# Four fixed PSUM banks for the seven-product units of an fp32 two-block transformer kernel

## The chip, the cores and the metric

The kernel runs on one core of a Trainium2 chip. The metric is the device time of one launch in microseconds, the median of several runs of the same program. A profile is one further execution, taken with the hardware profiler.

## What the reference computes

Two transformer blocks of width 1024 over 512 tokens, all in fp32. The first has two layers: a stick-breaking attention and a retention, each followed by a squared-ReLU MLP with 4096 hidden units. The second is a gated feed-forward, a mixer (a sparse attention beside an mLSTM), and a second gated feed-forward, each of the two with 2816 hidden units. What matters here are the up projections of these four feed-forward parts:

```python
def squared_relu_mlp(h, w_up, w_down):
    u = jax.nn.relu(h @ w_up)
    return (u * u) @ w_down
...
def swiglu_ffn(x, g, w_gate, w_up, w_down):
    h = rms_norm_2(x, g)
    return (jax.nn.silu(h @ w_gate) * (h @ w_up)) @ w_down
```

## The kernel before

Everything is kept transposed: a tile is 128 features by 512 tokens. An fp32 product is made of three TensorE passes over operands that are split in a high and a low part (`mm3`, L125 to L129: high by low, low by high, high by high), so each weight tile is cast to its high part on ScalarE and its low part is the difference, made on VectorE. The engines' names are those of the profile: PE is TensorE, ACT is ScalarE, DVE is VectorE, SP the queue that issues most transfers, POOL GpSimd.

**Dense units.** `g_unit` (L286) makes one 128 by 512 output tile in one PSUM bank: 8 feature tiles, 3 passes of 512 columns each, 24 matmuls. It takes its bank from the tag `m` (3 banks). Only the first three units of the first gated feed-forward take theirs from the tag `z` (4 banks), which `SPARE = 3` says. The eighth bank has the tag `o` and serves small jobs.

**Seven-product units.** Most of the up projections (groups 1 to 3 of 4 in each MLP, the gate and up pairs 4 to 21 of 22 in each gated feed-forward) are made by Strassen's scheme in Winograd's form: a pair of output tiles with its tokens halved is a 2 by 2 block product, made with seven half-sized products in place of eight. There are 12 such units in each MLP and 18 in each gated feed-forward, 60 in all. `w_unit` (L330) runs one: seven products x = 0 to 6 of 4 feature tiles by 3 passes, so 84 matmuls of 256 columns. The products accumulate on each other. The unit has one bank `a` of tag `m`, with c11 in its left half and p5 in its right half, and one bank of tag `z` with c in its left and b in its right half. Product 0 goes to c11, 1 to p5, 2 to b, 3 to c11, 4 to c, 5 to b, 6 to c. Between products ACT copies partial results, in `between(x)`, which stands after the second of a product's four feature tiles:

- x = 1, L342: b is set to c11 (as it is after product 0), PSUM to PSUM;
- x = 2, L344: p5 is copied to SBUF, as s5;
- x = 3, L346: c is set to b (after product 2), PSUM to PSUM;
- x = 5, L348: c (after product 4) is copied to SBUF, as s3.

At the end the four results are c11, b + s5, c and p5 + s3. `pair_done` (L553 in the MLP, L1002 in the gated feed-forward) takes them out of PSUM four steps after the unit's end (`later`, LAG = 4; a step is half a product of the next unit), applies the nonlinearity and splits the result into high and low parts for the down projection. Units take `z` banks in turn from two that `w_banks` (L296) sets aside at the start of the part, and `m` banks in turn from three. `w_banks` writes each of its banks once with a matmul that starts a group, so that later matmuls without a start flag add to what ACT has put there.

**Weights.** `prep` (L218) is called once a product, after the second feature tile. It casts weights up to five products ahead: ACT writes the high part (L274 for seven-product weights, L242 for dense ones), DVE the low part (L234, L243), and DVE makes two of the sums of weight blocks (L265). The other sums come from transfers that POOL issues with an add.

**Order.** The text of the kernel gives every instruction its priority. The tile framework's planner then lays out each engine's queue and adds the waits, and it moves instructions past each other where one would wait: in the trace the matmuls of one product are interrupted by some of another unit's. Each engine runs its queue in order. An instruction that writes a PSUM bank waits until another engine has finished with that bank.

Of the kernel before, what the change touches and what calls it, by code (L numbers as in the profile page):

```python
# [11 lines left out]
AF = mybir.ActivationFunctionType  # L12
ALU = mybir.AluOpType
# [28 lines left out]
ML = 2  # L42
AT = 2
ZT = 1
SPARE = 3
S1 = 16
S2 = 18
GAS = 1
# [39 lines left out]
class Builder:  # L88
    def __init__(self, tc, d, out, pools):
        self.tc, self.nc, self.d, self.out = tc, tc.nc, d, out  # L90
        self.cp, self.wp, self.hp, self.sp, self.pp = pools
        self.seq = []
        self.subs = []
        self.spare = 0
        self.pend = []
        self.n = 0
        self.pos = 0
        self.raw_at = 0
        self.prep_at = 0
        self.raws = {}  # L100
        self.sums = {}
        self.whi = {}
        self.wraw = set()
        self.ready = {}
        self.uid = 0
        self.stop_at = None
# [178 lines left out]

    def g_unit(self, name, X, w=None):  # L286
        w = w or self.next(name)
        ps = self.ps("z" if self.spare > 0 else "m")
        self.spare -= 1
        n = len(X)  # L290
        for k in range(n):
            self.mm3(ps, w[:, k * 128:(k + 1) * 128], X[k], k == 0, k == n - 1)
            yield
        self.last = ps

    def w_banks(self, any512):  # L296

        out = []
        for _ in range(2):
            b = self.ps("z")  # L300
            self.nc.tensor.matmul(b, self.onesr, any512, start=True, stop=True)
            out.append(b)
        return out

    def w_operands(self, X, T, lift):
# [21 lines left out]
                      "t2": p2[:, lo], "t3": p2[:, hi]})  # L327
            yield

    def w_unit(self, name, T, bank):  # L330


        nc = self.nc
        lo, hi = slice(0, 256), slice(256, 512)
        a = self.ps("m")
        c11, p5, c, b = a[:, lo], a[:, hi], bank[:, lo], bank[:, hi]
        s = self.h()
        s5, s3 = s[:, lo], s[:, hi]

        def between(x):  # L340
            if x == 1:
                nc.scalar.activation(b, c11, AF.Copy)  # L342
            elif x == 2:
                nc.scalar.activation(s5, p5, AF.Copy)  # L344
            elif x == 3:
                nc.scalar.activation(c, b, AF.Copy)  # L346
            elif x == 5:
                nc.scalar.activation(s3, c, AF.Copy)  # L348

        for x, (dst, (_, y)) in enumerate(zip((c11, p5, b, c11, c, b, c), WOPS)):  # L350
            w = self.next(name)
            for k in range(4):
                self.mm3(dst, w[:, k * 128:(k + 1) * 128], T[k][y], x == 0 and k == 0, k == 3, skip=True)
                if k == 1:
                    between(x)
                    self.prep()
                if k % 2:
                    yield
        self.last = (c11, (b, s5), c, (p5, s3))

    def g_tokens(self, name, X, done):

# [176 lines left out]
    def mlp(self, layer, hh, X, box, nxt):  # L539

        nc = self.nc
        st = {}
        self.norm_soon(st, box)
        U = {}


        def up_done(m, ps):
            z = self.h()
            nc.scalar.activation(z, ps, AF.Relu)
            nc.scalar.activation(z, z, AF.Square)  # L550
            U[m] = self.split(z)

        def pair_done(m, p):  # L553
            c11, c12, c21, c22 = p
            lo, hi = slice(0, 256), slice(256, 512)
            y, z = self.h(), self.h()
            nc.vector.tensor_tensor(y[:, hi], c12[0], c12[1], ALU.add)
            nc.vector.tensor_tensor(z[:, hi], c22[0], c22[1], ALU.add)
            nc.scalar.activation(y[:, lo], c11, AF.Relu)
            nc.scalar.activation(z[:, lo], c21, AF.Relu, scale=-1.0)  # L560
            nc.vector.scalar_tensor_tensor(y, y, 0.0, y, ALU.max, ALU.mult)
            nc.scalar.activation(z[:, hi], z[:, hi], AF.Relu, scale=-1.0)
            nc.scalar.activation(z, z, AF.Square)
            U[m] = self.split(y)
            U[m + 1] = self.split(z)

        def down_done(grp, m, ps):
            if "R2" not in st:
                st["R2"] = self.h()
                nc.vector.tensor_tensor(st["R2"], st["R"], st["R"], ALU.mult)  # L570
            t = self.h()
            nc.vector.tensor_tensor(t, ps, st["R2"], ALU.mult)  # L572
            nc.vector.tensor_tensor(hh[m], hh[m], t, ALU.add)
            if grp == 3:
                nxt(m)

        T = []
        ops = self.w_operands(X, T, lambda k: self.lifted(hh[k], self.g(f"mlp{layer}", k)))
        banks = self.w_banks(X[0].hi)

        def main():
            for grp in range(4):
                for m in range(0, 8, 2):
                    if grp == 0:
                        for x in range(2):
                            yield from self.g_unit(f"up{layer}", X[::2] + X[1::2])
                            self.later(up_done, m + x, self.last)
                    else:
                        yield from self.w_unit(f"up{layer}", T, banks[m // 2 % 2])
                        self.later(pair_done, m, self.last)  # L590
                if grp == 0:
                    for _ in ops:
                        pass
                self.flush()
                W = [U[m] for m in range(8)]
                for m in range(8):
                    yield from self.g_unit(f"dn{layer}", W)
                    self.later(down_done, grp, m, self.last)

        self.weave(main(), [[ops, WT]])  # L600
        self.flush()

# [385 lines left out]
    def ffn(self, which, hh, X, st, nxt, lift, after=lambda: None):  # L988
# [3 lines left out]
        U = {}  # L992
# [6 lines left out]
            nc.vector.tensor_tensor(z, pu, z, ALU.mult)  # L999
            U[i] = self.split(z)  # L1000

        def pair_done(i, p):  # L1002
            c11, c12, c21, c22 = p
            R = st["R"]
            lo, hi = slice(0, 256), slice(256, 512)
            z, u = self.h(), self.h()
            nc.vector.tensor_tensor(z[:, hi], c12[0], c12[1], ALU.add)
            nc.vector.tensor_tensor(z[:, lo], c11, R[:, lo], ALU.mult)
            nc.vector.tensor_tensor(z[:, hi], z[:, hi], R[:, hi], ALU.mult)
            nc.scalar.activation(z, z, AF.Silu)  # L1010
            nc.vector.tensor_tensor(u[:, hi], c22[0], c22[1], ALU.add)
            nc.vector.scalar_tensor_tensor(u[:, lo], c21, -1.0, z[:, lo], ALU.mult, ALU.mult)
            nc.vector.scalar_tensor_tensor(u[:, hi], u[:, hi], -1.0, z[:, hi], ALU.mult, ALU.mult)  # L1013
            U[i] = self.split(u)

        def down_add(m, ps, c):
            t = self.h()
# [12 lines left out]
        def main():  # L1030
            for gi, grp in enumerate((range(0, 8), range(8, 16), range(16, 22))):
                for i in grp:
                    if i < GC:
                        yield from self.g_unit(f"gu{which}", X[::2] + X[1::2])
                        pg = self.last
                        yield from self.g_unit(f"gu{which}", X[::2] + X[1::2])
                        self.later(up_done, i, pg, self.last)
                        if i == GC - 1:
                            for _ in ops:
                                pass  # L1040
                            after()
                    else:
                        yield from self.w_unit(f"gu{which}", T, banks[i % 2])
                        self.later(pair_done, i, self.last)
                self.flush()
                W = [U[i] for i in grp]
                tail = gi == 2 and which == 2
                for m in range(7 if tail else 8):
                    yield from self.g_unit(f"fd{which}" if gi < 2 else f"fe{which}", W)
                    self.later(down_done, gi == 2, m, self.last)  # L1050
                if tail:

                    w = self.next(f"fe{which}")
                    for a, b in ((0, 256), (256, 512)):
                        ps = self.ps("m")
                        for k in range(6):
                            self.mm3(ps[:, a:b], w[:, k * 128:(k + 1) * 128], [x[:, a:b] for x in W][k], k == 0, k == 5)
                            yield
                        down_add(7, ps, slice(a, b))
                        nc.sync.dma_start(out=self.out[7][:, a:b], in_=hh[7][:, a:b])  # L1060
# [592 lines left out]
    def build(self):  # L1653
# [121 lines left out]
                nc.vector.scalar_tensor_tensor(hh[kt], hh[kt], self.g("fin", kt), R1, ALU.mult, ALU.mult)  # L1775
        self.later(two_norms, lag=N1)
        self.later(spread_r, lag=N2)
        self.spare = SPARE
        X, Y = [], X
        self.ffn(1, hh, Y, st, ready("mixn", X, hh), lambda k: self.lifted(hh[k], self.gg[:, k:k + 1]), residual)  # L1780
        if stop == "ffn1":
# [162 lines left out]
```

## Time and profile before

| | |
|---|---|
| median of 3 runs | 2537.15 us (2536.19 to 2539.76) |
| the profiled execution, device time | 2539.24 us |
| its span, first to last instruction | 2537.5 us |
| mean granted TensorE clock | 0.997 of full speed |
| PE busy, share of the span | 99% |
| DVE, ACT busy | 68%, 50% |

The profile's PE durations overlap: a matmul's row lasts longer than the time until the next one may start, so a PE that is busy for 99% of the span can still lose time. What a matmul costs is read from the distance between the starts of two neighbours. PE is the matmul itself and PEld the load of its stationary operand, which normally runs ahead of it.

### The profile page before, as it was taken

The numbers are of one execution on the slowest core, as the hardware profiler recorded it, in microseconds if no ns is written. First come the engines' busy times: TensorE is split into PE (matmuls) and PEld (weight loads), VectorE is DVE, ScalarE is ACT, GpSimd is POOL, SyncE is SP. The second block draws the span as 40 slices with busy tenths as digits, with TensorE's granted clock in tenths as the row PEclk, the third lists the DMA queues.
The fourth block names the chain that finished last, engine by engine and source line by source line (L and its number), as shares of the span: only waits on it lengthen the run. The fifth ranks groups of instructions, "written<-read, shape, count | busy, mean of one in ns | idle before, by whom it ended". The sixth has DMA issues, their size and how long they took to land.

```text
span 2537.5 us, 35245 instructions
## 1 busy us (share of the span) xinstructions
PE 2501.1 (99%) x13679; PEld 2148.6 (85%) x13679; DVE 1719.4 (68%) x3061; ACT 1259.9 (50%) x2160; POOL 138.1 (5%) x242
## 2 busy tenths in 40 slices
PE   9999999999999999999999999999999999999999
PEld 7888788888888888888888888888877888889888
DVE  7877856656555555656657766667899677666665
ACT  6777745435333323535536444445556454544443
POOL 0000000010000000000010001010000000001010
PEclk9999999999999999999999999999999999999999
DMA  4112144453322222244352445453221112445451
GB/s 168 67 50 84 67 121 138 116 143 115 109 74 84 87 83 88 83 121 150 114 149 100 128 134 144 148 134 112 71 83 67 67 67 83 111 147 146 147 136 71
DMA packets 78512, 273.20 MB, mean 108 GB/s; under 512 B 8836, under 2 KB 9220, under 8 KB 60680
## 3 DMA queue, kind: packets, MB, share of 16 engines
q1 hardware_dynamic: 60912, 239.43, 26.8%
q0 software_dynamic: 17280, 31.46, 7.5%
q8 instruction: 107, 1.75, 0.3%
q14 instruction: 61, 0.50, 0.1%
q10 hardware_dynamic: 152, 0.06, 0.0%
HBM read 268.82 MB, written 2.10 MB: 107 GB/s over the span
## 4 chain that ended last, share of the span: by engine, by line
PE 91%; DVE 4%; ACT 3%; issue 1%; DMA 0%; SPq 0%; ACTq 0%; DVEq 0%
PE ps_m L127 23%; PE ps_m L128 22%; PE ps_m L129 22%; PE ps_z L127 7%; PE ps_z L129 6%; PE ps_z L128 6%; ACT whi L242 1%; PE ps_z L789 1%; PE ps_z L136 1%; PE ps_z L790 1%; PE ps_o L437 1%; PE ps_z L137 1%; DVE wlo L243 1%; PE ps_o L444 1%; DVE h L1385 0%
## 5 line engine op out<-in xcount | busy, mean ns | idle before, releaser
L127 PE MATMUL ps_m<-h,whi 128*128 128x512 f32 (+1 forms) x2450 | 925.4, 379 | 13.2 <-ACT ps_z L342 3.9
L128 PE MATMUL ps_m<-h,wlo 128*128 128x512 f32 (+1 forms) x2450 | 919.0, 375 | 2.1 <-DVE wlo L234 2.1
L129 PE MATMUL ps_m<-h,whi 128*128 128x512 f32 (+1 forms) x2450 | 917.8, 375 | 0.0
L242 ACT ACTIVATE whi<-raw 128x1024 fp32r<-128x1024 f32 (+2 forms) x297 | 309.8, 1043 | 569.7 <-PE ps_m L129 463.8
L127 PEld LDWEIGHTS ps_m<-h,whi 128*128 128x128 f32 x2450 | 462.4, 189 | 104.1 <-ACT ps_z L342 6.9
L129 PEld LDWEIGHTS ps_m<-h,whi 128*128 128x128 f32 x2450 | 462.2, 189 | 81.4 <-issue 0.2
L128 PEld LDWEIGHTS ps_m<-h,wlo 128*128 128x128 f32 x2450 | 462.8, 189 | 77.9 <-DVE wlo L234 3.2
L243 DVE TENSOR_TENSOR wlo<-raw,whi 128x1024 fp32r<-128x1024 f32 (+2 forms) x297 | 356.8, 1201 | 161.6 <-ACT whi L242 148.3
L274 ACT ACTIVATE wlo<-raw 128x512 fp32r<-128x512 f32 x120 | 75.4, 630 | 175.4 <-PE ps_m L128 128.7
L175 DVE TENSOR_TENSOR h<-h 128x512 fp32r<-128x512 f32 (+1 forms) x172 | 114.8, 685 | 56.3 <-ACT h L174 55.4
L127 PE MATMUL ps_z<-h,whi 128*128 128x256 f32 (+1 forms) x504 | 149.6, 297 | 0.5 <-ACT ps_z L346 0.5
L174 ACT ACTIVATE h<-h 128x512 fp32r<-128x512 f32 (+1 forms) x172 | 105.1, 624 | 88.2 <-DVE h L1013 28.7
L129 PE MATMUL ps_z<-h,whi 128*128 128x256 f32 (+1 forms) x504 | 145.1, 288 | 0.0
L128 PE MATMUL ps_z<-h,wlo 128*128 128x256 f32 (+1 forms) x504 | 144.9, 288 | 0.0
L127 PE MATMUL ps_z<-h,wlo 128*128 128x256 f32 x480 | 141.0, 294 | 0.0
L129 PE MATMUL ps_z<-h,wlo 128*128 128x256 f32 x480 | 135.7, 283 | 0.0
L128 PE MATMUL ps_z<-h,whi 128*128 128x256 f32 x480 | 135.6, 282 | 0.0
L572 DVE TENSOR_TENSOR h<-ps_m,h 128x512 f32<-128x512 f32 x64 | 44.2, 691 | 131.4 <-PE ps_m L129 131.4
L234 DVE TENSOR_TENSOR wlo<-raw,wlo 128x512 fp32r<-128x512 f32 x120 | 82.4, 687 | 49.5 <-ACT wlo L274 48.5
L127 PE MATMUL ps_m<-h,wlo 128*128 128x256 f32 x360 | 105.1, 293 | 4.6 <-ACT ps_z L342 4.5
L127 PEld LDWEIGHTS ps_z<-h,whi 128*128 128x128 f32 x504 | 96.0, 191 | 11.0 <-ACT h L348 6.0
L128 PE MATMUL ps_m<-h,whi 128*128 128x256 f32 x360 | 102.2, 285 | 1.2 <-DVE whi L234 1.2
(346 smaller groups left out, 4138.9 us busy)
## 6 DMA issues: line engine op xcount, KB each, us to landing
raw<-dn SPq DMA_DIRECT2D x32, 1024.0 KB, 4.8
raw<-gu SPq DMA_DIRECT2D x72, 256.0 KB, 3.9
raw<-gu SPq DMA_DIRECT2D x36, 512.0 KB, 4.4
raw<-fd SPq DMA_DIRECT2D x16, 1024.0 KB, 4.8
raw<-up SPq DMA_DIRECT2D x48, 256.0 KB, 3.6
raw<-up SPq DMA_DIRECT2D x24, 512.0 KB, 4.4
raw<-gu POOLq DMA_DIRECT2D x36, 256.0 KB, 4.1
h<-gu SPq DMA_DIRECT2D x36, 256.0 KB, 4.7
```

The costliest lines, as they stand in the source:

```text
L127: mm(ps, lhs.hi, rhs.lo, start=first, stop=False, skip_group_check=skip)
L128: mm(ps, lhs.lo, rhs.hi, start=False, stop=False, skip_group_check=skip)
L129: mm(ps, lhs.hi, rhs.hi, start=False, stop=last, skip_group_check=skip)
L136: mm(ps, stack, rhs.lo, start=first, stop=False)
L137: mm(ps, stack, rhs.hi, start=False, stop=last)
L174: self.nc.scalar.activation(p.hi, x, AF.Copy)
L175: self.nc.vector.tensor_tensor(p.lo, x, p.hi.bitcast(F32), ALU.subtract)
L234: nc.vector.tensor_tensor(lo, src, hi.bitcast(F32), ALU.subtract)
L242: nc.scalar.activation(hi[:, a:b], r[:, a:b], AF.Copy)
L243: nc.vector.tensor_tensor(lo[:, a:b], r[:, a:b], hi[:, a:b].bitcast(F32), ALU.subtract)
L274: self.nc.scalar.activation(t[:, 0:512], src, AF.Copy)
L572: nc.vector.tensor_tensor(t, ps, st["R2"], ALU.mult)
```

## The change

The unit has four banks of tag `z`, one for each of c11 (`a`), p5 (`p`), b and c, of which the left half is used, and the same four serve all units of a part. The tag `m` is left to the dense units. Products 0 and 1 start a group in their own bank, so only b and c need the matmul of `w_banks`. The copies stand ahead of a product's first matmul, in `before(x)`. `pair_done` now returns four functions, of which three run inside the unit: c11 is taken out at x = 4, b + s5 and p5 + s3 at x = 6; the rest (c, the second half of the nonlinearity, both splits) runs one step after the unit's end. `SPARE` is gone, and every dense unit takes a bank of tag `m`.

```diff
     def g_unit(self, name, X, w=None):
         w = w or self.next(name)
-        ps = self.ps("z" if self.spare > 0 else "m")
-        self.spare -= 1
+        ps = self.ps("m")
...
     def w_banks(self, any512):
-        out = []
-        for _ in range(2):
-            b = self.ps("z")
+        out = [self.ps("z") for _ in range(4)]
+        for b in out[2:]:
             self.nc.tensor.matmul(b, self.onesr, any512, start=True, stop=True)
-            out.append(b)
         return out
...
-    def w_unit(self, name, T, bank):
+    def w_unit(self, name, T, banks, done):
         nc = self.nc
-        lo, hi = slice(0, 256), slice(256, 512)
-        a = self.ps("m")
-        c11, p5, c, b = a[:, lo], a[:, hi], bank[:, lo], bank[:, hi]
+        n = slice(0, 256)
+        a, p, b, c = [t[:, n] for t in banks]
         s = self.h()
-        s5, s3 = s[:, lo], s[:, hi]
+        s5, s3 = s[:, n], s[:, 256:512]
-        def between(x):
+        def before(x):
             if x == 1:
-                nc.scalar.activation(b, c11, AF.Copy)
+                nc.scalar.activation(b, a, AF.Copy)
             elif x == 2:
-                nc.scalar.activation(s5, p5, AF.Copy)
+                nc.scalar.activation(s5, p, AF.Copy)
             elif x == 3:
                 nc.scalar.activation(c, b, AF.Copy)
+            elif x == 4:
+                done[0](a)
             elif x == 5:
                 nc.scalar.activation(s3, c, AF.Copy)
+            elif x == 6:
+                done[1](b, s5)
+                done[2](p, s3)
-        for x, (dst, (_, y)) in enumerate(zip((c11, p5, b, c11, c, b, c), WOPS)):
+        for x, (dst, (_, y)) in enumerate(zip((a, p, b, a, c, b, c), WOPS)):
             w = self.next(name)
+            before(x)
             for k in range(4):
-                self.mm3(dst, w[:, k * 128:(k + 1) * 128], T[k][y], x == 0 and k == 0, k == 3, skip=True)
+                self.mm3(dst, w[:, k * 128:(k + 1) * 128], T[k][y], x < 2 and k == 0, k == 3, skip=True)
                 if k == 1:
-                    between(x)
                     self.prep()
                 if k % 2:
                     yield
-        self.last = (c11, (b, s5), c, (p5, s3))
+        self.later(done[3], c, lag=1)
...
-        def pair_done(m, p):
-            c11, c12, c21, c22 = p
+        def pair_done(m):
             lo, hi = slice(0, 256), slice(256, 512)
             y, z = self.h(), self.h()
-            nc.vector.tensor_tensor(y[:, hi], c12[0], c12[1], ALU.add)
-            nc.vector.tensor_tensor(z[:, hi], c22[0], c22[1], ALU.add)
-            nc.scalar.activation(y[:, lo], c11, AF.Relu)
-            nc.scalar.activation(z[:, lo], c21, AF.Relu, scale=-1.0)
-            nc.vector.scalar_tensor_tensor(y, y, 0.0, y, ALU.max, ALU.mult)
-            nc.scalar.activation(z[:, hi], z[:, hi], AF.Relu, scale=-1.0)
-            nc.scalar.activation(z, z, AF.Square)
-            U[m] = self.split(y)
-            U[m + 1] = self.split(z)
+            def d11(c11):
+                nc.scalar.activation(y[:, lo], c11, AF.Relu)
+            def d12(p, q):
+                nc.vector.tensor_tensor(y[:, hi], p, q, ALU.add)
+                nc.vector.scalar_tensor_tensor(y, y, 0.0, y, ALU.max, ALU.mult)
+            def d22(p, q):
+                nc.vector.tensor_tensor(z[:, hi], p, q, ALU.add)
+            def d21(c21):
+                nc.scalar.activation(z[:, lo], c21, AF.Relu, scale=-1.0)
+                nc.scalar.activation(z[:, hi], z[:, hi], AF.Relu, scale=-1.0)
+                nc.scalar.activation(z, z, AF.Square)
+                U[m] = self.split(y)
+                U[m + 1] = self.split(z)
+            return d11, d12, d22, d21
...
-                        yield from self.w_unit(f"up{layer}", T, banks[m // 2 % 2])
-                        self.later(pair_done, m, self.last)
+                        yield from self.w_unit(f"up{layer}", T, banks, pair_done(m))
...
-        self.spare = SPARE
```

The gated feed-forward's `pair_done` is cut in the same way: d11 multiplies c11 by the norm's row (DVE), d12 adds b and s5, multiplies, and takes the Silu of the gate, d22 adds p and s3, and d21 makes the two products of up and gate and the split.

## Rows read from the trace of the kernel before

**Rows 1.** The page: busy time by engine, and the chain that ended last.
```profile
PE 2501.1 (99%) x13679; PEld 2148.6 (85%) x13679; DVE 1719.4 (68%) x3061; ACT 1259.9 (50%) x2160; POOL 138.1 (5%) x242
...
PE 91%; DVE 4%; ACT 3%; issue 1%; DMA 0%; SPq 0%; ACTq 0%; DVEq 0%
```

**Rows 2.** Busy time by stretch: the twelve with seven-product units (three shown), and their sum.
```profile
470.20:516.00 45.80, 44.96 (x345) 42.27 (x344) 30.99 (x48) 30.08 (x60) 1.73 (x2) 1.00 0.42 132
...
1451.50:1497.10 45.60, 44.33 (x345) 41.87 (x344) 37.09 (x64) 26.69 (x50) 1.72 (x2) 1.00 0.42 133
1539.30:1628.90 89.60, 87.30 (x679) 82.59 (x678) 65.69 (x119) 52.47 (x100) 8.63 (x10) 1.00 0.52 151
...
sum 678.80, PE 664.08 PEld 626.57 DVE 481.40 ACT 415.85 POOL 42.08; mean PE 55.34 PEld 52.21 DVE 40.12 ACT 34.65 POOL 3.51
```
A line has the stretch, its length, then busy time (and instructions) of PE, PEld, DVE, ACT and POOL, the granted clock, and the DMA engines' share and rate.

**Rows 3.** Timeline of one unit in the first gated feed-forward: PE and ACT.
```profile
1562.67 0.61 ACT L274 ACTIVATE whi<-raw 128x512 fp32r<-128x512 f32 x1
...
1562.96 0.28 PE L127 MATMUL ps_m<-h,wlo 128*128 128x256 f32 x1
...
1563.19 0.37 ACT L342 ACTIVATE ps_z<-ps_m 128x256 f32<-128x256 f32 x1
...
1563.61 0.38 PE L127 MATMUL ps_m<-h,wlo 128*128 128x256 f32 x1 [0.37 <-ACT ps_z L342]
...
1563.83 0.28 PE L128 MATMUL ps_m<-h,wlo 128*128 128x256 f32 x1
...
1565.73 0.28 PE L129 MATMUL ps_z<-h,whi 128*128 128x256 f32 x1
...
1566.05 0.37 ACT L346 ACTIVATE ps_z<-ps_z 128x256 f32<-128x256 f32 x1 [0.35 <-PE ps_z L129]
...
1566.21 0.28 PE L128 MATMUL ps_m<-h,wlo 128*128 128x256 f32 x1
...
1566.47 0.39 PE L127 MATMUL ps_z<-h,whi 128*128 128x256 f32 x1
...
1566.70 0.28 PE L128 MATMUL ps_z<-h,whi 128*128 128x256 f32 x1
...
1571.03 0.28 PE L128 MATMUL ps_z<-h,wlo 128*128 128x256 f32 x1
...
1573.54 0.28 PE L128 MATMUL ps_m<-h,whi 128*128 128x256 f32 x1
```
A line has start and length in us, engine, line and operation; in brackets the engine's idle time before it and what ended it.

**Rows 4.** Who waited for whom, PEld and PE: us in total, times, longest.
```profile
PEld ps_m L127 <- ACT ps_z L342: 16.1, 37, 0.7
PEld ps_z L127 <- ACT h L348: 11.8, 58, 0.2
PEld ps_z L127 <- ACT ps_z L346: 9.2, 41, 0.7
...
PEld ps_m L127 <- ACT whi L242: 4.4, 10, 0.5
...
PEld ps_m L128 <- DVE wlo L234: 3.2, 6, 0.5
PEld ps_m L128 <- DVE whi L234: 2.7, 7, 0.4
...
PE ps_m L127 <- ACT ps_z L342: 8.4, 23, 0.5
```

**Rows 5.** Groups of DVE instructions in the stretch 470.2 to 516 us.
```profile
L561 DVE SCALAR_TENSOR_TENSOR h<-h 128x512 f32<-128x512 f32 x3 | 2.1, 684 | 0.0
...
L557 DVE TENSOR_TENSOR h<-ps_z,h 128x256 f32<-128x256 f32 x3 | 1.3, 425 | 0.2
```
A line has the count, then busy us and mean ns of one, then the engine's idle us before them.

**Rows 6.** Timeline at the start of the first gated feed-forward: PE and DVE.
```profile
1417.92 0.49 PE L127 MATMUL ps_m<-h,whi 128*128 128x512 f32 x1
...
1420.74 0.68 DVE L997 TENSOR_TENSOR h<-ps_z,h 128x512 f32<-128x512 f32 x1
...
1422.37 0.39 PE L127 MATMUL ps_z<-h,whi 128*128 128x512 f32 x1
```

More of the change, by code (lines that the diff above doesn't have):

```diff
@@ L44 @@
 ZT = 1
-SPARE = 3
 S1 = 16
@@ L93, in __init__ @@
         self.subs = []
-        self.spare = 0
         self.pend = []
@@ L1000, in up_done, with pair_done, d11, d12 @@
             U[i] = self.split(z)
-        def pair_done(i, p):
-            c11, c12, c21, c22 = p
+        def pair_done(i):
+            lo, hi = slice(0, 256), slice(256, 512)
             R = st["R"]
-            lo, hi = slice(0, 256), slice(256, 512)
             z, u = self.h(), self.h()
[L1007 to L1014, printed above, removed]
+            def d11(c11):
+                nc.vector.tensor_tensor(z[:, lo], c11, R[:, lo], ALU.mult)
+            def d12(p, q):
+                nc.vector.tensor_tensor(z[:, hi], p, q, ALU.add)
+                nc.vector.tensor_tensor(z[:, hi], z[:, hi], R[:, hi], ALU.mult)
+                nc.scalar.activation(z, z, AF.Silu)
+            def d22(p, q):
+                nc.vector.tensor_tensor(u[:, hi], p, q, ALU.add)
+            def d21(c21):
+                nc.vector.scalar_tensor_tensor(u[:, lo], c21, -1.0, z[:, lo], ALU.mult, ALU.mult)
+                nc.vector.scalar_tensor_tensor(u[:, hi], u[:, hi], -1.0, z[:, hi], ALU.mult, ALU.mult)
+                U[i] = self.split(u)
+            return d11, d12, d22, d21
         def down_add(m, ps, c):
@@ L1042, in main @@
                     else:
-                        yield from self.w_unit(f"gu{which}", T, banks[i % 2])
-                        self.later(pair_done, i, self.last)
+                        yield from self.w_unit(f"gu{which}", T, banks, pair_done(i))
                 self.flush()
```

## The prediction

> **What bounds the kernel.** I read the page first, then busy time by stretch, a timeline inside one stretch, the table of waits, and last the groups of DVE instructions. By the page the chain that ended last lies on PE for 91% of the span, DVE and ACT together take 7%, and PE is busy for 99% while DVE and ACT have room [rows 1]. So a change pays only where PE loses time between matmuls, and the busy share hides that, because rows of pipelined matmuls overlap. The distance between starts shows it. In an undisturbed run 22 matmuls of 256 columns start between 1571.03 and 1573.54 us: 21 steps of 0.1195 us [rows 3].
>
> The change touches the seven-product units alone, and these lie in twelve stretches (six of four units in the MLPs, in each gated feed-forward one of four, one of eight, one of six), 678.8 us in sum [rows 2]. Their 60 units have 60 x 84 = 5040 matmuls of 256 columns, which need 5040 x 0.1195 = 602 us. Each stretch also holds some seven to ten dense matmuls that the planner moved in (345 in the first row of [rows 2] less 4 x 84 leaves 9), over twelve stretches some 95, which at the distance of 0.23 us that [rows 6] show for 512 columns (1417.92 to 1422.37 in 19 steps) make 22 us. What is left, 678.8 - 602 - 22 = 55 us, is time in which PE started nothing. No gain inside the units can be larger than about 55 us.
>
> **Where the 55 us go.** The timeline shows the two kinds of stop [rows 3]. The large one: ACT begins the copy L342 of c11 at 1563.19, after a weight cast (L274) that began at 1562.67; PE's last start before it is at 1562.96, the next is at 1563.61, when the copy is through. That is 0.65 us in place of 0.12. The matmuls released there are those of product 1, which write p5, a half of the bank that the copy does not read: they wait for the bank, not for data. After such a stop the next load is exposed as well (1563.61 to 1563.83, 0.22 in place of 0.12). One stop costs 0.53 + 0.10 = 0.63 us. The small one: L346 holds back a matmul from 1566.21 to 1566.47, and the next start is at 1566.70: 0.14 + 0.11 = 0.25 us. The planner had put matmuls of another unit ahead of it, so most of the wait was already filled.
>
> The table of waits counts them [rows 4]. L342 stops the load 37 times, and 23 times so long that the matmul row too shows idle time: 23 x 0.63 + 14 x 0.25 = 18 us. L348 (58 times) and L346 (41 times) at 0.25 us: 14.5 + 10.3 = 25 us. Together 43 us by this count. From the other side: late weights (L242, and L234 twice) account for 4.4 + 3.2 + 2.7 = 10.3 us, with 13 exposed loads behind L234 some 11.6 us, and 55 - 11.6 = 43. Both ways are rough by 2 us. I take 42 us for waits on the four copies' banks.
>
> **The change, part by part.**
>
> *Four banks.* A product never writes a bank that is being copied. The copy of c11 to b must be done when product 2 starts, no longer while product 1 runs; c from b is needed by product 4, with product 3 in between; s3 leaves c while product 5 writes b. Each copy gets one product of cover. From the last start of a product to the first start that needs its copy there are 13 steps, 1.55 us. The hand-off takes: last start to copy 0.32 us (1565.73 to 1566.05), copy 0.37 us, and 0.05 us until PE goes on (1566.42 to 1566.47) [rows 3]: 0.74 us. That leaves 0.81 us. A cast in hand at that moment delays the copy by up to 0.61 us (L274): still hidden. Two casts one behind the other, 1.2 us, make PE 0.4 us late, 0.5 with the exposed load. Bounds: all 42 us gone, or half of some 150 copies late by 0.25 us as now, some 20 us left. I take 3 us left, because ACT is busy for 52.5 of 89.6 us in a stretch [rows 2] and the copy stands ahead of the casts of its product in the text.
>
> *Waits that stay.* Nothing removes the 11.6 us of late weights directly. But they come about where the planner has pulled matmuls forward into a stop (a product that is begun early holds its weights' buffers longer, and the casts wait for buffers). With fewer stops to fill, part should go. Bounds 0 and 11.6; I take 4.
>
> *Extraction inside the unit.* The same instructions, moved: none is added or removed on ACT or DVE. They stand ahead of the casts of products 4 and 6 in the text, so on ACT and DVE later casts queue behind them, at most 0.42 + 0.68 + 0.42 = 1.5 us on DVE (L557 twice, L561) [rows 5]. Those casts are for products up to five ahead, more than 7 us of PE time, which hides it; without that cover it would be up to 1.5 us in each of 60 units. No transfer is issued there, and the order on SP's and POOL's queues stays. The pool tiles taken a unit earlier cost nothing unless that pool is empty, and no wait in [rows 4] is on it.
>
> *One set for all units.* This adds waits. The next unit's product 1 starts a group in p, so the DVE read of p + s3 must be over; before, the units took turns among five banks. The read follows product 5: 0.32 us, then the DVE work of 1.5 us, with one cast in hand 0.69 us more (the longest kind, as L561), 2.5 us. Product 1 of the next unit starts after products 6 and 0, 25 steps or 2.99 us. It fits, by 0.5 us. Behind that matmul all of PE would wait. The copy that overwrites b needs the read of b, which comes first, and c and a have two products of room. I take 0 and give the other end as a rival.
>
> *`w_banks` and `SPARE`.* Four calls with two matmuls each, before and after: 0. The first gated feed-forward's fourth dense unit now needs the bank that DVE L997 reads at 1420.74 [rows 6]. There the trace already has a dense unit in `m` at 1417.92 while another waits for a `z` bank until 1422.37. With three `m` banks the third unit starts at about 1417.9 and runs for 24 x 0.23 = 5.5 us, to 1423.4, and L997 ends at 1421.4. So 0; if L997 were later by 4 us, 2 us.
>
> **Sum.** -42 + 3 - 4 = -43 us. The profiled execution took 2539.2 us (1.7 more than its span), so 2496 us in its terms. The median of the runs is 2.1 us lower: 2494 us.
>
> **A rule against it.** DVE is busy for 65.7 us of a stretch of 89.6 [rows 2], so reads can queue, yet no wait of PE on a DVE read of a bank stands in [rows 4]. The Trainium skill, "Perfetto Trace Analysis", section "Matmul Optimizations", asks that all eight PSUM banks be used. By that rule the step from five banks in turn to four fixed ones goes the wrong way, and the time is that of the single-set rival below. The same page, section "Matmuls", lets independent groups rotate through banks so that the evacuation of one overlaps the next; by that the change is right. The trace of before has only PE held up by copies in a shared bank, which is for the second.
>
> **Rivals.**
>
> - *Copies late (chance 0.13).* ACT, or the planner's order on it, puts two casts ahead of a copy often enough that 20 to 30 us of the 42 stay. For it: in [rows 3] the copy L342 did stand behind a cast. Against: one cast is covered. Time: 42 - 20 to 30 + 4 leaves a gain of 16 to 26 us, 2511 to 2521.
> - *Single set, slower (0.05).* The read of p + s3 comes late because DVE has several casts in hand. It costs nothing until DVE is 0.5 us later than worked out, and eats the whole gain when each unit loses 42/60 = 0.7 us more. With four casts of 0.69 us in hand in place of one the read ends at 4.6 us, 1.6 us late, with the exposed load 1.7 in each unit: 60 x 1.7 = 102 us, less 43, about 2595 us; two casts in hand give 0.2 late and 18 us, 2512. Four are unlikely with DVE idle for a quarter of the stretch.
> - *No change (0.06).* PE's time comes back as waits for weights: ACT to DVE to PE becomes the limit. It would need DVE to be busy all the time; 65.7 us for eight units are 8.2 us for a unit that would take 84 x 0.1195 = 10.04. Time: 2537.
> - *Everything (0.04).* The late weights and all stops go: 55 us, 2482.
>
> **How the numbers follow.** The forecast has 0.72, with a range of its own of 2486 to 2508 (a gain of 51: no copy late and 9 of the 11.6 us gone; a gain of 29: 13 us of late copies and none of the 11.6 gone). Left out above 2518 are the two rivals at no change and slower and part of the late copies, 0.15, and below 2484 0.03: the range is 2484 to 2518. A change of 0.2% (5 us) is about what a measurement can tell here. Faster by more: 0.72 + 0.13 + 0.04, that is 0.89; within: 0.05; slower: 0.06.
>
> **What would show it.** Right: the waits on L342, L346 and L348 (by their new lines) nearly vanish from the list of PE and PEld; the stretch of eight units shrinks from 89.6 to about 83 us; matmuls of a product follow each other in order, with no other unit's in between; the stretches' busy time on ACT and DVE stays. Wrong: a wait of PE on a DVE instruction that reads a bank; waits on casts longer than now; casts of 0.61 us directly ahead of most copies with a PE wait behind them; or a loss outside the twelve stretches, above all at the start of the first gated feed-forward.

## The result, and the profile after

The median is 2482.82 us (2482.13 to 2484.37, 4 runs) against 2538.45 us before (2536.19 to 2539.86, 4 runs): the ratio is 0.9783, 95% interval 0.9766 to 0.9799, 55.6 us less. The direction is as forecast, the size is not: the forecast was 2494 us, the range 2484 to 2518, and the time is that of the rival "everything" (2482 us, chance 0.04). The profiled execution took 2483.38 us, with a span of 2481.7 us.

In the changed kernel the lines have moved: the three passes of `mm3` are L125 to L127, the copies L337 (c11 to b), L339 (s5), L341 (b to c) and L345 (s3), the weight casts L272 on ACT and L232 on DVE. The page, busy time and chain:

```profile
PE 2458.5 (99%) x13679; PEld 2141.8 (86%) x13679; DVE 1723.5 (69%) x3061; ACT 1253.1 (50%) x2160; POOL 138.1 (6%) x242
...
PE 93%; DVE 3%; ACT 2%; issue 1%; DMA 0%; SPq 0%; DVEq 0%; ACTq 0%
```

Nothing in the busy shares tells of a gain of 2%: against [rows 1] PE is at 99% both times. The stretches tell it (busy time by stretch, columns as in [rows 2]):

```profile
467.80:508.00 40.20, 40.20 (x337) 40.19 (x335) 32.29 (x51) 30.03 (x62) 1.72 (x2) 1.00 0.47 151
...
1430.00:1471.70 41.70, 40.49 (x338) 40.29 (x337) 37.63 (x67) 26.26 (x51) 1.72 (x2) 1.00 0.46 146
1515.40:1595.90 80.50, 80.50 (x673) 80.50 (x672) 67.35 (x122) 51.57 (x101) 8.63 (x10) 1.00 0.58 167
...
sum 604.60, PE 603.39 PEld 603.08 DVE 497.50 ACT 411.41 POOL 42.09; mean PE 50.28 PEld 50.26 DVE 41.46 ACT 34.28 POOL 3.51
```

The twelve stretches take 604.6 us in place of 678.8 [rows 2]. They no longer hold dense matmuls (336 or 672 of the unit's own, give or take one at the edges), which were 22 us of the 678.8. So the units need 604.6 us where they needed about 657, and 5040 matmuls at 0.1195 us are 602: of the 55 us of stops 52 to 53 are gone. What is left is mostly in the second stretch shown, the first unit of the first gated feed-forward. The list of who waited for whom has one entry of PEld on a copy, where [rows 4] have 136:

```profile
PEld ps_z L125 <- ACT h L345: 1.4, 1, 1.4
```

The waits for late weights inside the stretches are gone as well, and in all twelve stretches the twelve matmuls of each product follow each other with none of another product in between.

The remaining 3 us of the difference between the two spans (55.8) lie outside the stretches and have two sources. One is the end of each stretch: before, a load some 4 us after it waits 0.2 to 0.3 us for the split of the last unit's results (L175, in the changed kernel L173); after, two such waits are left (before, then after; the wait of 0.9 stands elsewhere):

```profile
PEld ps_m L127 <- DVE h L175: 3.9, 13, 0.9
```

```profile
PEld ps_m L125 <- DVE h L173: 0.3, 2, 0.2
```

By the distances between starts in the 10 us behind each stretch this brings 1.6 us in all. The other is the granted clock. From the end of the last stretch of the first gated feed-forward to the first of the second it is 477.2 us before and 475.7 after, and 474.7 and 478.3 in two of the kernels below (`spare0` and `between`). In this part the granted clock falls to 0.50 (the lower level, 1.2 GHz) during or right behind 24 matmuls of 2 columns; the spell lasts 10.2 us before and in `between`, 3.4 us after and in `spare0` (columns as in [rows 2], before, then after):

```profile
1964.20:1974.40 10.20, 10.20 (x33) 8.65 (x33) 6.18 (x15) 2.75 (x5) 0.41 (x2) 0.50 0.00 0
```

```profile
1928.50:1931.80 3.30, 3.30 (x9) 2.54 (x9) 2.58 (x4) 1.85 (x4) 0.41 (x2) 0.50 0.00 0
```

There matmuls of 512 columns start 0.43 us apart in place of 0.23, and by starts the long spell costs 5.0 us, the short one 1.5. Two other spells (near 280 us in both, near 1890 us before and 1850 after) are longer after than before, which takes back 2.1 us. So some 1.4 us of the difference is the clock in the two executions that were profiled, and no run ties it to the change.

One hand-off in the changed kernel (timeline, PE and ACT):

```profile
1546.94 0.28 PE L127 MATMUL ps_z<-h,wlo 128*128 128x256 f32 x1
...
1547.06 0.28 PE L125 MATMUL ps_z<-h,whi 128*128 128x256 f32 x1
1547.17 0.63 ACT L172 ACTIVATE h<-h 128x512 fp32r<-128x512 f32 x1 [0.55 <-DVE h L1027]
...
1547.71 0.37 ACT L337 ACTIVATE ps_z<-ps_z 128x256 f32<-128x256 f32 x1
...
1548.38 0.28 PE L127 MATMUL ps_z<-h,whi 128*128 128x256 f32 x1
1548.50 0.28 PE L125 MATMUL ps_z<-h,wlo 128*128 128x256 f32 x1
```

Product 0 has its last start at 1546.94, product 1 runs on at once, the copy stands behind a 0.63 us ACT instruction and is through at 1548.08, and product 2, which needs it, starts at 1548.50 without a pause, 0.42 us after the copy's end. In [rows 3] the same copy behind the same kind of instruction stopped PE for 0.5 us.

### The profile page after: what moved, and what is told of

The parts are those of the page before. It is cut to its first block, busy times and chain, and to the rows that moved or that the text cites. A ratio compares the mean times of both kernels' runs of the same rounds, so it can differ in the third digit from the quotient of the medians.

```text
span 2481.7 us, 35229 instructions
## 1 busy us (share of the span) xinstructions
PE 2458.5 (99%) x13679; PEld 2141.8 (86%) x13679; DVE 1723.5 (69%) x3061; ACT 1253.1 (50%) x2160; POOL 138.1 (6%) x242
## 4 chain that ended last, share of the span: by engine, by line
PE 93%; DVE 3%; ACT 2%; issue 1%; DMA 0%; SPq 0%; DVEq 0%; ACTq 0%
PE ps_m L125 20%; PE ps_m L126 20%; PE ps_m L127 20%; PE ps_z L125 9%; PE ps_z L127 9%; PE ps_z L126 9%; PE ps_z L134 1%; PE ps_z L796 1%; PE ps_o L437 1%; DVE wlo L241 1%; PE ps_z L135 1%; PE ps_z L797 1%; PE ps_o L444 1%; ACT whi L240 0%; DVE h L1399 0%
## 5 line engine op out<-in xcount | busy, mean ns | idle before, releaser
L125 PE MATMUL ps_m<-h,whi 128*128 128x512 f32 (+1 forms) x2114 | 831.2, 393 | 7.1 <-DVE h L1191 3.5
L126 PE MATMUL ps_m<-h,wlo 128*128 128x512 f32 (+1 forms) x2114 | 826.0, 391 | 0.0
L127 PE MATMUL ps_m<-h,whi 128*128 128x512 f32 (+1 forms) x2114 | 825.0, 390 | 0.0
L125 PEld LDWEIGHTS ps_m<-h,whi 128*128 128x128 f32 x2114 | 398.1, 188 | 89.3 <-issue 6.6
L127 PEld LDWEIGHTS ps_m<-h,whi 128*128 128x128 f32 x2114 | 398.1, 188 | 83.3
L126 PEld LDWEIGHTS ps_m<-h,wlo 128*128 128x128 f32 x2114 | 398.5, 189 | 76.9 <-issue 1.2
L125 PE MATMUL ps_z<-h,whi 128*128 128x256 f32 x840 | 237.8, 283 | 1.2 <-ACT h L345 1.2
L125 PE MATMUL ps_z<-h,wlo 128*128 128x256 f32 x840 | 237.7, 283 | 0.0
L126 PE MATMUL ps_z<-h,wlo 128*128 128x256 f32 x840 | 237.7, 283 | 0.0
L127 PE MATMUL ps_z<-h,whi 128*128 128x256 f32 x840 | 237.7, 283 | 0.0
L127 PE MATMUL ps_z<-h,wlo 128*128 128x256 f32 x840 | 237.7, 283 | 0.0
L126 PE MATMUL ps_z<-h,whi 128*128 128x256 f32 x840 | 237.7, 283 | 0.0
L125 PEld LDWEIGHTS ps_z<-h,whi 128*128 128x128 f32 x840 | 161.2, 192 | 1.8 <-ACT h L345 1.4
L126 PEld LDWEIGHTS ps_z<-h,whi 128*128 128x128 f32 x840 | 161.2, 192 | 0.4
L125 PEld LDWEIGHTS ps_z<-h,wlo 128*128 128x128 f32 x840 | 161.3, 192 | 0.0
L126 PEld LDWEIGHTS ps_z<-h,wlo 128*128 128x128 f32 x840 | 161.3, 192 | 0.0
L127 PEld LDWEIGHTS ps_z<-h,wlo 128*128 128x128 f32 x840 | 161.3, 192 | 0.0
L127 PEld LDWEIGHTS ps_z<-h,whi 128*128 128x128 f32 x840 | 161.2, 192 | 0.0
L272 ACT ACTIVATE wlo<-raw 128x512 fp32r<-128x512 f32 x120 | 75.0, 625 | 148.8 <-PE ps_m L126 127.9
```

What stands on the lines that cost most here:

```text
L125: mm(ps, lhs.hi, rhs.lo, start=first, stop=False, skip_group_check=skip)
L126: mm(ps, lhs.lo, rhs.hi, start=False, stop=False, skip_group_check=skip)
L127: mm(ps, lhs.hi, rhs.hi, start=False, stop=last, skip_group_check=skip)
L272: self.nc.scalar.activation(t[:, 0:512], src, AF.Copy)
```

## Experiments

Two theories stood against each other. *Banks*: PE stops because a matmul waits until another engine has finished with the bank that it writes; four banks take that wait away. *Order*: the earlier place of the copies and the extraction brings the gain. A third question was why the late weights went. All medians stand beside a run of the kernel before on the same chip (2538 to 2540 us); ratios are to that.

**spare0.** The kernel before with one constant changed.

```diff
-SPARE = 3
+SPARE = 0
```

> The kernel before, with the one constant SPARE at 0: all dense units take their bank from the tag of three. If my sum is right, the first three dense units of the first gated feed-forward neither wait nor gain: 2538 us, within 3 us. If the shift of the early units into the other tag was worth the part of the gain that lies outside the seven-product stretches (3 us), it shows here as 2535 us.

Measured: 2537.69 us, ratio 0.9998 (0.9989 to 1.0007). The dropped `SPARE` is worth nothing that can be measured.

**oldbanks.** The changed kernel's order on the old banks.

```diff
-        a, p, b, c = [t[:, n] for t in banks]
+        m = slice(256, 512)
+        left, right = self.ps("m"), banks[0]
+        banks.append(banks.pop(0))
+        a, p, b, c = left[:, n], left[:, m], right[:, m], right[:, n]
```

(with two banks in `w_banks`, and the start flag at product 0 alone)

> The changed kernel's order (copies ahead of a product, extraction inside the unit) on the banks of the kernel before: c11 and p5 share one, b and c share one, units take turns. Theory banks (a matmul waits for another engine's use of its bank): the stops stay and some grow, since the extraction of b + s5 now also reads the bank that product 6 writes: 2540 to 2590 us. Theory order (the earlier place of copies and extraction brings the gain): 2483 to 2500 us.

Measured: 2541.93 us, ratio 1.0015 (1.0005 to 1.0024). Theory order falls: its part of the change alone brings no gain (by starts it saves 1.7 us at the ends of the stretches and loses 6 us more inside them). Waits of PEld (L348 is the copy of c to s3, L340 that of c11 to b, the others are casts):

```profile
PEld ps_z L125 <- ACT h L348: 11.8, 58, 0.2
PEld ps_m L125 <- ACT ps_z L340: 11.7, 18, 0.7
PEld ps_m L125 <- ACT wlo L272: 7.5, 11, 0.7
...
PEld ps_m L125 <- ACT whi L240: 6.4, 6, 1.2
PEld ps_m L125 <- ACT whi L272: 4.4, 6, 0.7
```

The copies still stop PE, and more waits are for late weights (18.3 us in these rows, 10.3 in [rows 4]).

**p_apart.** The kernel before, with p5 alone in a bank of its own; copies and extraction as before.

```diff
-SPARE = 3
+SPARE = 0
...
-        c11, p5, c, b = a[:, lo], a[:, hi], bank[:, lo], bank[:, hi]
+        c11, p5, c, b = a[:, lo], bank[1][:, lo], bank[0][:, lo], bank[0][:, hi]
```

(`w_banks` makes two pairs, and product 1 starts a group too)

> The kernel before with p5 alone in a bank of its own (two in turn), the copies and the extraction at their old places, b and c still in one bank. Theory banks: the waits behind the copy of c11 go (18 to 20 us), those behind the other copies stay: 2515 to 2522 us, and some of the late weights' 11.6 us may go with them. Theory order: no change, 2538 us.

Measured: 2494.81 us, ratio 0.9831 (0.9815 to 0.9847): a gain of 43 us, about twice the 16 to 23 us that were expected. Of the waits on copies one kind is left, that for the copy of c to s3 (here L346), the only copy that still shares its bank with the product that runs meanwhile:

```profile
PEld ps_z L127 <- ACT h L346: 11.9, 58, 0.3
```

The waits for the copy of b to c (9.2 us in [rows 4]) went with those for the copy of c11, and so did the late weights. In [rows 3] one sees how they hang together: product 3 writes c11, whose bank is being read for s5, so the planner put the first three matmuls of product 4 ahead of it (1566.47), and these need the copy of b to c sooner. With p5 in another bank product 3 need not wait and covers that copy: in this run's stretch of eight units one product 3 starts at 1523.48 directly behind product 2, the copy (L344) at 1523.68, and product 4 at 1524.92.

**c_apart.** The same for c.

```diff
-        c11, p5, c, b = a[:, lo], a[:, hi], bank[:, lo], bank[:, hi]
+        c11, p5, c, b = a[:, lo], a[:, hi], bank[1][:, lo], bank[0][:, lo]
```

(`SPARE = 0`, two pairs in `w_banks`)

> The kernel before with b and c in banks of their own (two sets in turn), the copies and the extraction at their old places, c11 and p5 still in one bank. Theory banks: the waits behind the copy of c to SBUF go, about 12 to 15 us, and those behind the copy of c11 stay: 2523 to 2527 us. Theory order: no change, 2538 us.

Measured: 2505.51 us, ratio 0.9872 (0.9857 to 0.9886): a gain of 33 us where 11 to 15 were expected, again more than the waits on that one copy. Waits of PEld (L340 copies c11 to b, L344 b to c):

```profile
PEld ps_m L127 <- ACT ps_z L340: 10.6, 45, 0.7
...
PEld ps_z L127 <- ACT ps_z L344: 3.5, 12, 0.7
...
PEld ps_m L127 <- ACT whi L242: 2.7, 6, 0.5
```

The copy of c to s3 is gone from the list, as theory banks says. The copy of c11 still stops PE, and some weights are still late. The two halves bring 43 + 33 = 76 us, the whole 55: part of the 55 us goes with either of them.

**between.** The changed kernel with `before(x)` called after the second feature tile, where the copies stood before.

```diff
             w = self.next(name)
-            before(x)
             for k in range(4):
...
                 if k == 1:
+                    before(x)
                     self.prep()
```

> The changed kernel with the copies and the extraction put back after the second feature tile of a product; banks as changed. The cover of a copy shrinks from 13 steps of 0.12 us to 7, 0.84 us, against a hand-off of 0.74 us plus whatever cast is in hand. If the place in the text binds the start of a copy, most copies behind a cast come 0.1 to 0.5 us late: 2495 to 2530 us. If the planner starts a copy when its data are there, wherever it stands, nothing changes: 2483 us, within 2.

Measured: 2482.30 us, ratio 0.9782 (0.9768 to 0.9797), and its stretches are as long as those of the changed kernel (40.2 and 80.6 us). The copies of c11 to b start 2.1 us after their unit's first matmul in both kernels (median of 60). A copy's place in the text does not bind its start; the planner starts it when its data are there.

**after_unit** and **after_unit2.** The changed kernel with the extraction one step after the unit's end. In the first all four results are taken there; c11 is then read when the next unit's product 0 has begun to overwrite it, so this kernel does not compute what the reference does; only its waits are of use. In the second c11 is taken inside the unit as changed.

```diff
-            elif x == 6:
-                done[1](b, s5)
-                done[2](p, s3)
...
-        self.later(done[3], c, lag=1)
+        def out():
+            done[1](b, s5)
+            done[2](p, s3)
+            done[3](c)
+        self.later(out, lag=1)
```

(the first also moves `done[0](a)`)

> The changed kernel with the whole extraction one step after the unit's end, none of it inside; banks and copies as changed. With one set of banks the next unit's product 1 then waits for the read of p. If that read starts only after the unit's end it ends about 0.7 + 0.3 + 1.5 us later against 1.5 us of cover, 1 us late in each of 60 units: about 2540 us. If DVE does the reads when their data are there, nothing changes: 2483 us.

> The changed kernel with c11 taken out inside the unit as changed, and the other three results one step after the unit's end. The next unit's copy into b and its product 1 in p then wait for the DVE reads of b and p. If the reads keep their place in time because their data are there before (p + s3 can be read from the end of the copy of c on, b + s5 from the end of product 5 on): 2483 us, within 3. If the reads start after the unit's end, they end some 0.7 + 0.3 + 0.8 us after it, and product 1, 1.4 us after it, waits 0.4 us or more in each of 60 units: 2505 us or more.

Measured: 2541.53 us, ratio 1.0014 (1.0005 to 1.0024), and 2482.96 us, ratio 0.9781 (0.9765 to 0.9798). In the first, PE waits for the late read of c11 (L1016, in the gated feed-forward; L559 in the MLP):

```profile
PEld ps_z L125 <- DVE h L1016: 30.7, 24, 1.3
PEld ps_z L125 <- ACT ps_z L337: 9.7, 13, 1.8
PEld ps_z L125 <- ACT h L559: 8.1, 12, 0.7
```

That is the price of the single-set rival, brought about by force: one result read after its bank's next turn has begun eats the whole gain. The cause is another than the rival's and than the expectation's: the late read is that of c11, not that of p + s3, and it is late by its place in the program, not because DVE is behind. In the second the reads of p + s3 (L1025) and b + s5 (L1020) come where they come in the changed kernel, 0.4 and 0.3 us later in the unit:

```profile
1553.79 0.42 DVE L1025 TENSOR_TENSOR h<-ps_z,h 128x256 f32<-128x256 f32 x1
1554.73 0.42 DVE L1020 TENSOR_TENSOR h<-ps_z,h 128x256 f32<-128x256 f32 x1
```

and in the changed kernel (L1023, L1018):

```profile
1553.43 0.42 DVE L1023 TENSOR_TENSOR h<-ps_z,h 128x256 f32<-128x256 f32 x1 [0.28 <-ACT h L345]
...
1554.46 0.42 DVE L1018 TENSOR_TENSOR h<-ps_z,h 128x256 f32<-128x256 f32 x1
```

So for these three results it does not matter whether the extraction is written inside the unit or just after.

**copies2, copies4.** The changed kernel with each copy done twice, and four times.

```diff
-                nc.scalar.activation(b, a, AF.Copy)
+                for _ in range(2):
+                    nc.scalar.activation(b, a, AF.Copy)
```

> The changed kernel with each of the four copies of a unit done twice (same data, same place). A hand-off grows from 0.74 to about 1.04 us, against 1.55 us of cover. If the slack that I worked out (0.81 us) is right: 2483 us, within 2. If ACT is short of time, 60 units times four copies of 0.3 us show in part: up to 2555 us.

> The changed kernel with each of the four copies done four times. A hand-off grows to about 1.65 us, against 1.55 us of cover: each of three copies per unit that PE needs comes at least 0.1 us late, 0.2 to 0.5 with the exposed load and a cast in hand: 60 times 3 times 0.2 to 0.5 is 36 to 90 us, 2519 to 2573 us. If the cover is larger than worked out: 2483 us.

Measured: 2509.33 us, ratio 0.9884 (0.9867 to 0.9900), and 2640.70 us, ratio 1.0405 (1.0389 to 1.0420). By the slack worked out the first should have cost nothing; it is some 26 us slower than the changed kernel, within what was allowed if ACT is short of time. The second lies far above its 2519 to 2573 us. With two copies (L338 is the copy of c11 to b), timeline of ACT and PE:

```profile
1546.28 0.37 ACT L338 ACTIVATE ps_z<-ps_z 128x256 f32<-128x256 f32 x1 [0.28 <-PE ps_z L127]
...
1546.56 0.62 ACT L272 ACTIVATE whi<-raw 128x512 fp32r<-128x512 f32 x1
...
1547.08 0.62 ACT L172 ACTIVATE h<-h 128x512 fp32r<-128x512 f32 x1
...
1547.40 0.28 PE L127 MATMUL ps_z<-h,wlo 128*128 128x256 f32 x1
...
1547.60 0.38 ACT L338 ACTIVATE ps_z<-ps_z 128x256 f32<-128x256 f32 x1
...
1548.03 0.39 PE L125 MATMUL ps_z<-h,whi 128*128 128x256 f32 x1 [0.35 <-ACT ps_z L338]
1548.25 0.28 PE L126 MATMUL ps_z<-h,whi 128*128 128x256 f32 x1
```

The planner did not put the two copies one behind the other: two other ACT instructions of 0.62 us stand in between here, and at least one does in 54 of the 60 units. PE starts at 1548.03 in place of 1547.52, 0.51 us late, and the next load costs 0.10 more. So a first copy and two casts ahead of a copy cost 0.6 us; less the 0.28 us from the first copy's start to the next ACT instruction's, two casts alone would cost some 0.3 (an estimate). The run does not measure the slack of a longer copy. The waits of PEld on that copy, with two copies and with four:

```profile
PEld ps_z L125 <- ACT ps_z L338: 18.9, 41, 0.6
```

```profile
PEld ps_z L125 <- ACT ps_z L338: 79.2, 56, 2.6
```

41 stops of 0.6 us are 25 us, about what the first kernel lost. With four copies each, PE waits for ACT in nearly every unit, so the cover has an end; by how much each of the longer hand-offs exceeds it was not worked out.

**halves5.** The kernel before with five weight buffers of each kind.

```diff
-HEAP = 70
-HALVES = 4
+HEAP = 64
+HALVES = 5
...
-        trace(tc, d, out)
+        trace(tc, d, out, stop="ffn1")
```

> The kernel before with five weight buffers of each kind in place of four. To make room the second block's mixer and its second gated feed-forward are left out and the general pool has 64 tiles, so only the stretches of seven-product units are compared, not the time. In an MLP stretch of the kernel before, waits for late weights cost 1.6 us of 3.7. If weights are late because products begun early hold buffers: below 0.5 us per stretch, and the waits on copies stay. If ACT and DVE are late with the casts for another reason: 1.6 us as before.

Measured: the MLP stretch corresponding to the first of [rows 2] takes 45.3 us in place of 45.8, with four or five more dense matmuls moved in (x350 in place of x345), and the stretch of eight units 86.6 us in place of 89.6. Busy time by stretch, and waits of PEld:

```profile
469.70:515.00 45.30, 45.29 (x350) 42.91 (x349) 31.09 (x47) 29.68 (x59) 1.73 (x2) 1.00 0.40 125
1528.90:1615.50 86.60, 86.57 (x682) 82.83 (x681) 65.99 (x118) 52.21 (x99) 8.65 (x10) 1.00 0.55 153
```

```profile
PEld ps_m L127 <- ACT ps_z L342: 8.4, 36, 0.5
PEld ps_z L127 <- ACT h L348: 6.6, 32, 0.3
...
PEld ps_z L127 <- ACT ps_z L346: 3.0, 15, 0.3
```

The three entries on late weights of [rows 4] (L242, and L234 twice) are gone, while the copies still stop PE: 36 waits on L342 in nine stretches. The kernel before has in the same nine stretches:

```profile
PEld ps_m L127 <- ACT ps_z L342: 8.4, 21, 0.7
PEld ps_z L127 <- ACT h L348: 8.1, 40, 0.2
PEld ps_z L127 <- ACT ps_z L346: 6.9, 30, 0.7
```

So the waits on copies went from 23.4 to 18.0 us, and those for late weights from 9.7 (L242 and L234 in the nine stretches) to none. The MLP stretch lost 45.3 - 336 x 0.1195 - 14 x 0.23 = 1.9 us, with 9 dense matmuls in [rows 2] 3.6. So the weights were late for want of buffers. The trace of the kernel before shows the same from the other end (timeline of PE, ACT, DVE and PEld):

```profile
405.32 0.28 PE L129 MATMUL ps_z<-h,wlo 128*128 128x256 f32 x1
...
405.64 0.63 ACT L274 ACTIVATE wlo<-raw 128x512 fp32r<-128x512 f32 x1 [0.81 <-PE ps_z L129]
...
406.31 0.68 DVE L234 TENSOR_TENSOR wlo<-raw,wlo 128x512 fp32r<-128x512 f32 x1
...
407.05 0.19 PEld L128 LDWEIGHTS ps_m<-h,wlo 128*128 128x128 f32 x1 [0.54 <-DVE wlo L234]
```

ACT stands idle until PE has finished with a product's weights at 405.32; only then does it cast the next ones, DVE makes their low part, and PE waits for that. In 22 of the 23 late weights of [rows 4] the chain leads back to PE in this way. Why single waits on the copy of c11 are shorter with five buffers (8.4 us are 36 waits, not 21) was not tried.

No kernel here beats the changed one by more than the noise (`between` and `after_unit2` are equal to it). Its stretches have some 2 us left to gain.

## Why the prediction was right and wrong

**What bounds the kernel, and the bound of 55 us: right.** Time without a start was worked out as 55 us, and 52 to 53 of it went. **Waits on banks, 42 us: right**, by `oldbanks` (order alone: no gain) and by `p_apart` and `c_apart`, where those copies leave the list that share a bank no longer. What does not hold is to price a single bank by the waits on its own copy, as the expectation of `p_apart` did: p5's bank was behind two of the three kinds of wait and behind the late weights, 43 us in place of 18 to 20.

**The step that failed is "Waits that stay".** I put 4 of 11.6 us for the late weights, and all of it went. The reason stood in that step, that products begun early hold their buffers, but only as something that accounts for a part. `halves5` shows that it accounts for the whole: one more buffer of each kind, with most of the stops on copies still there, clears the late weights. With no stop to fill the planner begins nothing early (336 matmuls in a stretch, no dense ones), and four buffers are enough. Those 7.6 us are most of what the forecast of 43 us missed. The Trainium skill, "Perfetto Trace Analysis", section "Optimization Strategy", says that the same gap repeated on the engine that should be saturated can mean too little SBUF or PSUM for the next tile. The traces of `halves5` and `p_apart` agree for both kinds of gap: one more weight buffer of each kind clears the one, and one more PSUM bank for each unit clears most of both.

**Copies late, 3 us: too much.** None is late but in one unit, the first of the first gated feed-forward, where the ACT instruction ahead of the copies itself waited 1.17 us for DVE. The hand-off shown above took what was worked out: one ACT instruction in hand, and 0.4 us left. `copies2` agrees roughly with the price of the rival (0.5 us with two casts ahead; some 0.3 by the estimate there), and in the changed kernel no copy is late for that reason. Together the two terms are -42 + 0 - 11.6 = -53.6 us, about what the stretches measure. The range ended too soon on this side because "everything" had 0.04: its two conditions were taken as separate luck, though both follow from the stops being gone. The rest of the 55.6 us, outside the stretches, the forecast did not have.

**One set for all units: right in the sum (0), wrong in the working.** The read of p + s3 does not follow product 5, as the place in the text has it, but the copy of s3, one product earlier: it starts at 1553.43, and the bank's next matmul at 1557.1 (product 1 of this unit began at 1547.06, and a unit is 84 steps of 0.1195 us). The margin is 3 us, not 0.5. The rule of the Trainium skill's "Perfetto Trace Analysis", section "Matmul Optimizations", to use all eight banks, did not decide here: both kernels hand out all eight (three, four and one), and the units went from five of them in turn to four fixed ones and gained. `after_unit` shows when a single set does cost: when a result is read after its bank's next turn has begun.

**`SPARE` and the place of the copies: right at 0**, by `spare0` and `between`; `w_banks` was not tried by itself. **Extraction inside the unit: 0 is right for its place in the unit**, by `after_unit2`, but the earlier extraction as a whole is worth 1.6 us: the waits for the last split at the ends of the stretches stand in the kernels that extract four steps after the unit's end (12 in `spare0`, as before) and are all but gone in those that extract at most one step after it (`oldbanks`, `between`, `after_unit2`). All else that the change brought is the work of the four banks.

Open: why the spells at half the clock last 3.4 us in one execution and 10.2 in another, and so why the part between the two gated feed-forwards varies by 3 us from kernel to kernel.

## What to carry to other kernels

Where PE is busy 99% of the time, compare the distance between starts with the undisturbed one, and multiply: what the stretch takes beyond that is the time there is to win, and the list of waits says from whom. When a planner fills a stop with other work, the stop has further costs elsewhere, in buffers held longer and in data needed sooner; a change that removes the stop takes these along, so waits that seem to have another cause should be counted with it when the range is set. Partial results that one engine reads while another writes the next belong in different banks, and a fixed set of banks will do if each is read before its next turn.
